# First operands loaded in pieces from two DMA queues, squares taken by pairs of tiles, outputs stored from two queues, and one GpSimd sum fewer

## The chip, the cores and the metric

The kernel runs on one core of one Trainium2 chip. The metric is device time in microseconds (us) of one execution, as a median over runs. The engines are named as the profile names them: PE (TensorE, the matrix engine), DVE (VectorE), ACT (ScalarE), POOL (GpSimd) and SP (SyncE, which here issues DMAs). PEld is the weight-load side of PE.

## The reference, cut to what matters

The input is x with 256 positions and 1024 features. The reference runs two mixers of a first block (a state-space mixer and a latent attention), a final norm, and then one layer of a second block: sparse attention and a convolution, a feed-forward part, a gate, and a last norm. Everything starts and ends with an RMS norm, and the change is at these two places:

```python
def rms_norm(x, w):
    xf = x.astype(jnp.float32)
    return (xf * lax.rsqrt(jnp.mean(xf * xf, axis=-1, keepdims=True) + RMS_EPS)).astype(x.dtype) * w
...
    for i in range(DEPTH):
        u = rms_norm(h, norm_w[i])
        y = ssd_mixer(u, ...)        # first step: u @ in_w
        h = h + y
...
    gate = jax.nn.sigmoid(rmsnorm(h, g_ple[i]) @ w_ple_gate[i])
    h = h + gate * (p[i] @ w_ple[i])
    return rmsnorm(h, g_final)
```

## The kernel before, in words

All activations are held transposed: `h` is 8 tiles of 128 features x 256 positions. A weight block is 128x1024, eight 128x128 tiles. Weights come from HBM in tiles named `raw` of up to 128x2048 (a ring of four buffers, line 176). To multiply at nearly full precision a weight is split into a rounded high part `whi` (ACT, line 182) and a remainder `wlo` (DVE, line 188), and three matmuls take the place of one. A few blocks are used whole, in plain float32 (`pj<-u,raw`). A float32 matmul shows as two PE rows, so a count in the timeline (x16) is twice that in the code.

**The start.** SP issues all DMAs, in program order: `n0` (the norm's weights, 4 KB), `h` in four pairs of tiles, and `raw` blocks of `w_si`, the first projection's weight. PE has nothing to work on yet and multiplies a tile of ones (`warm`, `WARM[0]` = 10 matmuls). The first projection does not wait for the norm: it multiplies `h` times `n0` without the factor 1/rms, and the factor is put on its result later (`r0b`). Function `first(k)` is the part of that projection that uses tile k of `h`: for k < 4 in float32 from `raw`, for k of 4 and over in three parts from `whi` and `wlo`. Meanwhile `square(k)` squares tile k on ACT and adds it to `ss` on DVE; `col_sum` sums `ss` over its 128 partitions with matmuls against ones into `st` (two matmuls, one for each half of the positions), and `mean_eps` and `rsqrt` make the factor `r0` from it on DVE, in steps on 128x2 values. `spread` turns `r0` into a tile `rb`. This stretch runs in an order written out by hand (`tc.manual_schedule`) on DVE, ACT and PE: `first(0)`, `first(1)`, `col_sum`, `first(2)`, `first(3)`, `spread`, and from there `first(4)` to `first(7)` beside the tiles `u` and their parts `uh` and `ul`. Then a scheduler orders the instructions. A side task (`dt_task`) makes small factors through a chain on DVE that ends in `av`, which PE needs for `pcum` (line 505).

**Waits on DMAs.** Each DMA signals its landing on one of eight counters, DMAHW0 to DMAHW7 in the listings, which are handed out in turn in program order over all queues. A DMA that gets a counter for the second time is issued only when the first DMA on it has landed; the queue behind it stands until then.

**`rsqrt`** is called ten times in the kernel. It starts from a guess made with integer operations (lines 257 and 258) and refines it.

**The end.** `gate_task2(m)` finishes tile m of `h` for the last norm and squares it. For m up to 6 the squares are summed on POOL (`fin.squares`, line 321) into `ssf`; tile 7 is done in two halves and its squares `sq7` go to `col_sum` themselves. On PE stand `warm` matmuls (`WARM[1]` = 6, then 1, then 6) between the `col_sum` calls, and after them come `mean_eps`, `rsqrt`, `spread`, five multiplications into `og` (line 1661) and five output DMAs from SP (line 1662).

Of the kernel before, what the change touches and what calls it, by code (L numbers as in the profile page):

```python
# [8 lines left out]
FT = mybir.dt.float32  # L9
# [7 lines left out]
S = 256  # L17
# [81 lines left out]
def build(tc, a, out):  # L99
# [54 lines left out]
    vec = const.tile([128, NVEC], FT, name="vec")  # L154
    cst = const.tile([128, NCST], FT, name="cst")
    n0 = const.tile([128, 8], FT, name="n0")
    nc.sync.dma_start(n0, a["n0"])
    nc.sync.dma_start(h[:, 0:2], a["xT"][:, 0:2])
    ones = const.tile([128, 128], FT, name="ones")
    nc.gpsimd.memset(ones, 1.0)  # L160

# [11 lines left out]
    def load(src):  # L173
        n = src.shape[-1]
        raw = wpool.tile([128, 2048], FT, name="raw", bufs=4)
        nc.sync.dma_start(raw[:, :n], src)
        return raw
# [73 lines left out]


    def rsqrt(x, n, y):
        t = small.tile([128, n], I32, name="rq_t")
        e = small.tile([128, n], FT, name="rq_e")
        c = small.tile([128, n], FT, name="rq_c")
        nc.vector.tensor_scalar(t, x.bitcast(I32), 1, None, op0=OP.logical_shift_right)
        nc.vector.tensor_scalar(y.bitcast(I32), t, -1, 0x5F3759DF, op0=OP.mult, op1=OP.add)

        nc.vector.tensor_mul(e, y, y)  # L260
        nc.vector.tensor_mul(e, e, x)
        nc.vector.tensor_scalar(e, e, 1.0, None, op0=OP.subtract)
        nc.vector.tensor_scalar(y, y, RSQRT[0], None, op0=OP.mult)
        nc.vector.scalar_tensor_tensor(c, e, RSQRT[1], e, op0=OP.add, op1=OP.mult)
        nc.vector.scalar_tensor_tensor(c, c, RSQRT[2], e, op0=OP.add, op1=OP.mult)
        nc.vector.scalar_tensor_tensor(c, c, RSQRT[3], e, op0=OP.add, op1=OP.mult)
        nc.vector.scalar_tensor_tensor(y, c, RSQRT[4], y, op0=OP.add, op1=OP.mult)

    def col_sum(o, s, start, stop=True):

        for b in range(2):
            mm(o[:, b:b + 1], s[:, b * 128:(b + 1) * 128], ones[:, 0:1], start and b == 0, stop)
# [83 lines left out]
        for _ in range(n):  # L356
            nc.tensor.matmul(p[:, :128], ones, ones, start=True, stop=True, skip_group_check=True)

    raws = [load(a["w_si"][:, :1024])]
    for i in range(1, 4):  # L360
        nc.sync.dma_start(h[:, 2 * i:2 * i + 2], a["xT"][:, 2 * i:2 * i + 2])
    raws += [load(a["w_si"][:, i * 1024:(i + 1) * 1024]) for i in (1, 2)]
# [11 lines left out]
    with tc.manual_schedule(engines={mybir.EngineType.DVE, mybir.EngineType.Activation, mybir.EngineType.PE}):  # L374
        pst = mx_ps("st")
        f0, x0, w0 = [], {}, {}
        ss = pa.tile([128, S], FT, name="ss", bufs=1)

        def square(k):
            s = ss if k == 0 else pa.tile([128, S], FT, name="sq0", bufs=2)  # L380
            nc.scalar.activation(s, h[:, k], AF.Square)
            if k:
                nc.vector.tensor_add(ss, ss, s)  # L383

# [17 lines left out]
        for k in range(4):  # L402
            u = pa.tile([128, S], FT, name="u0", tag="y", bufs=18)
            nc.vector.tensor_scalar(u, h[:, k], n0[:, k:k + 1], None, op0=OP.mult)
            f0.append(u)
            square(k)
        first(0)
        first(1)
        for k in range(4, 8):
            square(k)  # L410
        for k in range(4, 8):
            first_hi(k)
        col_sum(pst[:, :2], ss, True)
        first_lo(4)
        first_lo(5)
        m0 = small.tile([128, 2], FT, name="m0")
# [1195 lines left out]
    def gate_task2(m, p):  # L1612
# [1 line left out]
            yield 500  # L1614
        zh = pf.tile([128, S], FT, name="zh")
        if m == 7:
            last[0] = pf.tile([128, S], FT, name="sq7", bufs=1)

        for t in (slice(0, 128), slice(128, S)) if m == 7 else (slice(0, S),):
            nc.vector.scalar_tensor_tensor(zh[:, t], p[:, t], 0.5, r4b[:, t], op0=OP.mult, op1=OP.mult)  # L1620
# [3 lines left out]
            if m == 7:  # L1624
                nc.scalar.activation(last[0][:, t], h[:, m, t], AF.Square)
        done(p)
        if m < 7:
            fin.squares(m)

    last = [None]  # L1630
    w_pg = stream(a["w_pg"])
    w0 = [next(w_pg) for _ in range(4)]
    outs = four_ps(4)
# [9 lines left out]
    p = mx_ps("st")  # L1643
    warm(wp, WARM[1])
    col_sum(p[:, :2], fin.ss[0], True, False)
    warm(wp, WARM[2])
    col_sum(p[:, :2], last[0], False)
    warm(wp, WARM[3])
# [8 lines left out]
    p = mx_ps("spread")  # L1657
    spread(p, r5)
    m = 0
    for n in (1, 2, 2, 2, 1):  # L1660
        nc.vector.tensor_mul(og[:, m:m + n], og[:, m:m + n], p[:, None, :S].to_broadcast([128, n, S]))
        nc.sync.dma_start(out[:, m:m + n], og[:, m:m + n])
        m += n
    done(p)
    while pools:
# [131 lines left out]
```

## Time and profile before

| what | us |
|---|---|
| median of 3 runs | 863.78 (863.61 to 864.26) |
| the profiled execution's own time | 863.92 |
| its span in the profile | 862.0 |
| PE busy | 840.7 (98%) |
| DVE busy | 714.8 (83%) |
| ACT busy | 543.6 (63%) |
| PE busy in 0 to 20 us | 17.38 |
| PE busy in 841.5 to 862 us | 13.35 |

The span is what the profiler saw of the engines; 1.92 us of the execution's own time lie around it. Times in the sections below count from the start of the span. A busy PE is a PE with a matmul in its pipeline.

### The profile page before, as it was taken

What the parts mean: (1) busy time and instruction counts of PE and PEld (TensorE: products, weight loads), DVE (VectorE), ACT (ScalarE), POOL (GpSimd) and SP (SyncE); (2) the same over time, 40 slices, a digit from 0 to 9 for tenths busy, and PEclk for the clock granted to TensorE, in tenths of its full rate; (3) what the DMA queues carried; (4) which work ended last, traced back from release to release, by engine and by line L of the source; (5) the groups of instructions that cost most, each with busy time, mean ns of one, the idle gap of its engine ahead of it and who ended that gap; (6) DMA issues with size and microseconds to landing.
All of it is one profiled execution on the core that took longest, in us unless ns stands there. A gap on an engine that the chain in (4) does not pass through costs nothing.

```text
span 862.0 us, 17387 instructions
## 1 busy us (share of the span) xinstructions
PE 840.7 (98%) x6886; PEld 806.6 (94%) x6886; DVE 714.8 (83%) x1549; ACT 543.6 (63%) x1113; POOL 53.8 (6%) x66
## 2 busy tenths in 40 slices
PE   8999999999999999999999998998999999999996
PEld 8888999999999999999999887887999999999996
DVE  6999999788758888886679998965879988988756
ACT  5765766555647688786636465974558666656543
POOL 0000000110210000000330000001020000000102
PEclk9999999999999999999999998999999999999999
DMA  8424434444525335154343852335442655645601
GB/s 339 157 98 160 183 118 177 160 169 162 196 96 206 122 103 185 53 193 168 126 163 117 308 211 75 123 144 198 148 159 102 244 200 190 216 167 187 213 2 50
DMA packets 21681, 137.68 MB, mean 160 GB/s; under 512 B 2528, under 2 KB 3552, under 8 KB 6752
## 3 DMA queue, kind: packets, MB, share of 16 engines
q1 hardware_dynamic: 21600, 136.58, 43.7%
q8 instruction: 54, 0.88, 0.4%
q14 instruction: 27, 0.22, 0.1%
HBM read 135.52 MB, written 1.05 MB: 158 GB/s over the span
## 4 chain that ended last, share of the span: by engine, by line
PE 86%; DVE 5%; ACT 5%; DMA 1%; issue 1%; POOL 1%; SPq 0%; POOLq 0%; DVEq 0%; ACTq 0%
PE pj L146 54%; PE acc L146 10%; PE pz L146 10%; PE po L146 3%; PE ps L146 2%; DVE cv L1129 1%; ACT whi L182 1%; DVE wlo L188 1%; PE pt L150 1%; PE py L146 1%; ACT rope_t L800 1%; PE s L146 1%; DMA h<-in_xT 1%; PE pc L146 1%; DMA raw<-in_w_si 1%
## 5 line engine op out<-in xcount | busy, mean ns | idle before, releaser
L188 DVE TENSOR_TENSOR wlo<-raw,whi 128x1024 fp32r<-128x1024 f32 (+3 forms) x243 | 287.0, 1186 | 48.8 <-ACT whi L182 46.3
L182 ACT ACTIVATE whi<-raw 128x1024 fp32r<-128x1024 f32 (+3 forms) x243 | 247.0, 1025 | 108.7 <-PE pj L146 65.3
L146 PE MATMUL pj<-uh,whi 128*128 128x256 f32 x896 | 256.2, 287 | 2.6 <-DVE zh L1046 2.6
L146 PE MATMUL pj<-uh,wlo 128*128 128x256 f32 x896 | 253.6, 283 | 1.3 <-DVE wlo L188 1.2
L146 PE MATMUL pj<-ul,whi 128*128 128x256 f32 x896 | 252.8, 282 | 0.0
L146 PEld LDWEIGHTS pj<-uh,whi 128*128 128x128 f32 x896 | 169.7, 190 | 5.8 <-DVE zh L1046 2.8
L146 PEld LDWEIGHTS pj<-uh,wlo 128*128 128x128 f32 x896 | 170.1, 190 | 2.6 <-DVE wlo L188 2.1
L146 PEld LDWEIGHTS pj<-ul,whi 128*128 128x128 f32 x896 | 169.9, 190 | 0.6 <-issue 0.4
L146 PE MATMUL pz<-uh,whi 128*128 128x256 f32 x256 | 73.9, 288 | 0.4 <-ACT v L864 0.4
L146 PE MATMUL pz<-ul,whi 128*128 128x256 f32 x256 | 71.9, 281 | 0.0
L146 PE MATMUL pz<-uh,wlo 128*128 128x256 f32 x256 | 71.8, 280 | 0.0
L321 POOL TENSOR_TENSOR ss<-sqh,ss 128x256 f32<-128x256 f32 x35 | 30.1, 871 | 431.2 <-ACT sqh L320 430.7
L1129 DVE SCALAR_TENSOR_TENSOR cv<-cc,vec,cv 128x252 f32<-128x252 f32 (+28 forms) x120 | 50.0, 457 | 0.0
L146 PEld LDWEIGHTS pz<-uh,whi 128*128 128x128 f32 x256 | 48.3, 189 | 0.6 <-ACT v L864 0.6
L146 PEld LDWEIGHTS pz<-uh,wlo 128*128 128x128 f32 x256 | 48.3, 189 | 0.0
L146 PEld LDWEIGHTS pz<-ul,whi 128*128 128x128 f32 x256 | 48.2, 188 | 0.1
L1556 DVE SCALAR_TENSOR_TENSOR vo<-v,vec,vo 128x255 f32<-128x255 f32 (+1 forms) x88 | 41.7, 478 | 0.9
L534 DVE SCALAR_TENSOR_TENSOR cacc<-pj,cwh,cacc 128x253 f32<-128x253 f32 (+2 forms) x84 | 38.8, 473 | 2.2 <-ACT cacc L532 2.2
L146 PE MATMUL pj<-u,raw 128*128 128x256 f32 x128 | 31.2, 382 | 1.0 <-DMA raw<-in_w_si 1.0
L1554 ACT ACTIVATE vo<-v,vec 128x256 f32<-128x256 f32 x44 | 25.7, 590 | 3.4 <-DVE v L1551 3.3
L146 PEld LDWEIGHTS pj<-u,raw 128*128 128x128 f32 x128 | 22.9, 190 | 4.4 <-DVE ss L383 1.3
L900 ACT ACTIVATE P<-ps,nb,scq 128x128 f32<-128x128 f32 (+1 forms) x32 | 15.9, 507 | 14.7 <-DVE nb L898 14.7
(470 smaller groups left out, 2015.1 us busy)
## 6 DMA issues: line engine op xcount, KB each, us to landing
raw<-in_w_si SPq DMA_DIRECT2D x22, 1024.0 KB, 4.7
raw<-in_w_up SPq DMA_DIRECT2D x22, 1024.0 KB, 4.7
raw<-in_w_in SPq DMA_DIRECT2D x16, 1024.0 KB, 4.6
raw<-in_w_so SPq DMA_DIRECT2D x8, 1024.0 KB, 4.6
raw<-in_w_mz SPq DMA_DIRECT2D x8, 1024.0 KB, 4.6
raw<-in_w_mo SPq DMA_DIRECT2D x8, 1024.0 KB, 4.6
raw<-in_w_dn SPq DMA_DIRECT2D x8, 1024.0 KB, 4.7
raw<-in_w_mkv SPq DMA_DIRECT2D x4, 1024.0 KB, 4.7
```

What stands on the lines that cost most here:

```text
L146: nc.tensor.matmul(o, l, r, start=start, stop=stop, skip_group_check=True)
L150: nc.tensor.transpose(o, i, ident)
L182: nc.scalar.activation(hi[:, :n], raw, AF.Copy)
L188: nc.vector.tensor_sub(lo[:, :n], raw, hi[:, :n])
L321: nc.gpsimd.tensor_tensor(ss, s, ss, op=OP.add)
L534: nc.vector.scalar_tensor_tensor(acc[:, j:], p[:, :S - j], cwh[:, (3 - j) * 32 + f:(3 - j) * 32 + f + 1], acc[:, j:], op0=OP.mult, op1=OP.add)
L800: nc.scalar.activation(t[i ^ 32:(i ^ 32) + 32], src[i:i + 32], AF.Copy)
L900: nc.scalar.activation(P[:, c0:c0 + n], s[:, c0:c0 + n], AF.Exp, bias=nb[:, b:b + 1], scale=scq[:, b:b + 1], accum_out=sm[:, b:b + 1])
L1129: nc.vector.scalar_tensor_tensor(o[:, j:], c[:, :S - j], V("c31", (30 - j) * 4 + i), o[:, j:], op0=OP.mult, op1=OP.add)
L1554: nc.scalar.activation(o, v, AF.Identity, bias=V("fcb", f), scale=V("fcw", 88 + f))
L1556: nc.vector.scalar_tensor_tensor(o[:, j:], v[:, :S - j], V("fcw", (2 - j) * 44 + f), o[:, j:], op0=OP.mult, op1=OP.add)
```

## The change

The first weight block is loaded in two halves of 128x512 from ACT's DMA queue, while SP's queue starts with tile 0 of `h` instead of a pair, then `n0`, then tile 1. `square` now takes two tiles at a time, 128x512, so that four squares and three additions stand where eight and seven stood; `ss` and the squares take buffers of the later tiles `M` and `xdt`. `ss` is two tiles wide now, so `col_sum` is called twice at the start. In `rsqrt` the two integer steps become one, in all ten calls. At the end the squares of tile 6 are no longer added on POOL; they have a `col_sum` of their own. The outputs are stored from SP and ACT in turn.

```diff
--- before.py
+++ after.py
@@ -154,8 +154,13 @@
     vec = const.tile([128, NVEC], FT, name="vec")
     cst = const.tile([128, NCST], FT, name="cst")
     n0 = const.tile([128, 8], FT, name="n0")
+
+    raw0 = wpool.tile([128, 2048], FT, name="raw", bufs=4)
+    nc.scalar.dma_start(raw0[:, :512], a["w_si"][:, :512])
+    nc.sync.dma_start(h[:, 0:1], a["xT"][:, 0:1])
     nc.sync.dma_start(n0, a["n0"])
-    nc.sync.dma_start(h[:, 0:2], a["xT"][:, 0:2])
+    nc.scalar.dma_start(raw0[:, 512:1024], a["w_si"][:, 512:1024])
+    nc.sync.dma_start(h[:, 1:2], a["xT"][:, 1:2])
     ones = const.tile([128, 128], FT, name="ones")
     nc.gpsimd.memset(ones, 1.0)
 
@@ -251,11 +256,9 @@
 
 
     def rsqrt(x, n, y):
-        t = small.tile([128, n], I32, name="rq_t")
         e = small.tile([128, n], FT, name="rq_e")
         c = small.tile([128, n], FT, name="rq_c")
-        nc.vector.tensor_scalar(t, x.bitcast(I32), 1, None, op0=OP.logical_shift_right)
-        nc.vector.tensor_scalar(y.bitcast(I32), t, -1, 0x5F3759DF, op0=OP.mult, op1=OP.add)
+        nc.vector.tensor_scalar(y.bitcast(I32), x.bitcast(I32), -0.5, float(0x5F3759DF), op0=OP.mult, op1=OP.add)
 
         nc.vector.tensor_mul(e, y, y)
         nc.vector.tensor_mul(e, e, x)
@@ -356,7 +359,7 @@
         for _ in range(n):
             nc.tensor.matmul(p[:, :128], ones, ones, start=True, stop=True, skip_group_check=True)
 
-    raws = [load(a["w_si"][:, :1024])]
+    raws = [raw0]
     for i in range(1, 4):
         nc.sync.dma_start(h[:, 2 * i:2 * i + 2], a["xT"][:, 2 * i:2 * i + 2])
     raws += [load(a["w_si"][:, i * 1024:(i + 1) * 1024]) for i in (1, 2)]
@@ -374,11 +377,11 @@
     with tc.manual_schedule(engines={mybir.EngineType.DVE, mybir.EngineType.Activation, mybir.EngineType.PE}):
         pst = mx_ps("st")
         f0, x0, w0 = [], {}, {}
-        ss = pa.tile([128, S], FT, name="ss", bufs=1)
+        ss = pa.tile([128, 2, S], FT, name="ss", tag="M", bufs=3)
 
         def square(k):
-            s = ss if k == 0 else pa.tile([128, S], FT, name="sq0", bufs=2)
-            nc.scalar.activation(s, h[:, k], AF.Square)
+            s = ss if k == 0 else pa.tile([128, 2, S], FT, name="sq0", tag="xdt")
+            nc.scalar.activation(s, h[:, k:k + 2], AF.Square)
             if k:
                 nc.vector.tensor_add(ss, ss, s)
 
@@ -403,14 +406,16 @@
             u = pa.tile([128, S], FT, name="u0", tag="y", bufs=18)
             nc.vector.tensor_scalar(u, h[:, k], n0[:, k:k + 1], None, op0=OP.mult)
             f0.append(u)
-            square(k)
+            if k % 2:
+                square(k - 1)
         first(0)
         first(1)
-        for k in range(4, 8):
+        for k in (4, 6):
             square(k)
         for k in range(4, 8):
             first_hi(k)
-        col_sum(pst[:, :2], ss, True)
+        col_sum(pst[:, :2], ss[:, 0], True, False)
+        col_sum(pst[:, :2], ss[:, 1], False)
         first_lo(4)
         first_lo(5)
         m0 = small.tile([128, 2], FT, name="m0")
@@ -1614,7 +1619,7 @@
             yield 500
         zh = pf.tile([128, S], FT, name="zh")
         if m == 7:
-            last[0] = pf.tile([128, S], FT, name="sq7", bufs=1)
+            last[0] = pf.tile([128, S], FT, name="sq7", tag="sq7", bufs=2)
 
         for t in (slice(0, 128), slice(128, S)) if m == 7 else (slice(0, S),):
             nc.vector.scalar_tensor_tensor(zh[:, t], p[:, t], 0.5, r4b[:, t], op0=OP.mult, op1=OP.mult)
@@ -1624,10 +1629,13 @@
             if m == 7:
                 nc.scalar.activation(last[0][:, t], h[:, m, t], AF.Square)
         done(p)
-        if m < 7:
+        if m < 6:
             fin.squares(m)
-
-    last = [None]
+        elif m == 6:
+            last[1] = pf.tile([128, S], FT, name="sq6", tag="sq7", bufs=2)
+            nc.scalar.activation(last[1], h[:, m], AF.Square)
+
+    last = [None, None]
     w_pg = stream(a["w_pg"])
     w0 = [next(w_pg) for _ in range(4)]
     outs = four_ps(4)
@@ -1643,6 +1651,7 @@
     p = mx_ps("st")
     warm(wp, WARM[1])
     col_sum(p[:, :2], fin.ss[0], True, False)
+    col_sum(p[:, :2], last[1], False, False)
     warm(wp, WARM[2])
     col_sum(p[:, :2], last[0], False)
     warm(wp, WARM[3])
@@ -1657,9 +1666,9 @@
     p = mx_ps("spread")
     spread(p, r5)
     m = 0
-    for n in (1, 2, 2, 2, 1):
+    for i, n in enumerate((1, 2, 2, 2, 1)):
         nc.vector.tensor_mul(og[:, m:m + n], og[:, m:m + n], p[:, None, :S].to_broadcast([128, n, S]))
-        nc.sync.dma_start(out[:, m:m + n], og[:, m:m + n])
+        (nc.scalar if i % 2 else nc.sync).dma_start(out[:, m:m + n], og[:, m:m + n])
         m += n
     done(p)
     while pools:
```

At the start ACT's order, and what each row waits for, was this before:

```order
L381 ACT_TABLE_LOAD
L381 ACTIVATE ss<-h 128x256 [waits DMAHW1_49]
L381 ACTIVATE sq_127<-h 128x256
L381 ACTIVATE sq_132<-h 128x256 [waits DMAHW3_49]
L381 ACTIVATE sq_137<-h 128x256 [waits DVE_49]
L381 ACTIVATE sq_148<-h 128x256 [waits DMAHW4_49,DVE_49]
```

and is this after the change:

```order
L159 DMA raw<-in_w_si 128x512
L162 DMA raw<-in_w_si 128x512
L384 ACT_TABLE_LOAD [waits DMAHW4_49]
L384 ACTIVATE ss<-h 128x512 [waits DMAHW1_49]
L384 ACTIVATE sq_133<-h 128x512 [waits DMAHW5_49]
L384 ACTIVATE sq_144<-h 128x512 [waits DMAHW6_49]
L384 ACTIVATE sq_147<-h 128x512 [waits DMAHW7_49,DVE_49]
```

The load of ACT's function table stood first and free; it now stands behind two DMA issues and behind the wait for DMAHW4, the landing of tile 1 of `h`.

SP's first rows were these before (`n` is `n0`):

```order
L157 DMA n_76<-in_n 128x8
L158 DMA h<-in_xT 128x512
L176 DMA raw<-in_w_si 128x1024
L361 DMA h<-in_xT 128x512 x3
L176 DMA raw<-in_w_si 128x1024 x2
L363 DMA cst<-in_cst 128x384 [waits DMAHW0_49]
L176 DMA raw<-in_w_si 128x1024 [waits DMAHW1_49]
L365 DMA vec<-in_vec 128x669 [waits DMAHW2_49]
```

and these after:

```order
L160 DMA h<-in_xT 128x256
L161 DMA n_76<-in_n 128x8
L163 DMA h<-in_xT 128x256
L364 DMA h<-in_xT 128x512 x3
L181 DMA raw<-in_w_si 128x1024 [waits DMAHW0_49]
L181 DMA raw<-in_w_si 128x1024 [waits DMAHW1_49]
L366 DMA cst<-in_cst 128x384 [waits DMAHW2_49]
L181 DMA raw<-in_w_si 128x1024 [waits DMAHW3_49]
```

The next `raw` block, which was issued without a wait, now waits for DMAHW0 (the first half of the first block, from ACT's queue), and everything behind it on SP with it; the third waits for DMAHW1 (tile 0 of `h`), the fourth for DMAHW3 (the second half).

On DVE the place is the end of `first(7)`, where `pr`, the product of the first projection's result with `r0b`, waits for PE. Before:

```order
L292 TENSOR_TENSOR ul<-u,uh 128x256 [waits Activation_49]
L433 SCALAR_TENSOR_TENSOR u<-h,n_76,rb 128x256
L626 TENSOR_TENSOR pr<-pj,r0b 128x256 [waits PE_49]
L292 TENSOR_TENSOR ul<-u,uh 128x256 [waits Activation_49]
L433 SCALAR_TENSOR_TENSOR u<-h,n_76,rb 128x256
L534 SCALAR_TENSOR_TENSOR cacc<-pr,cwh,cacc 128x255 [waits Activation_49]
L626 TENSOR_TENSOR pr<-pj,r0b 128x256 [waits PE_49]
```

After:

```order
L295 TENSOR_TENSOR ul<-u,uh 128x256 [waits Activation_49]
L438 SCALAR_TENSOR_TENSOR u<-h,n_76,rb 128x256
L295 TENSOR_TENSOR ul<-u,uh 128x256 [waits Activation_49]
L438 SCALAR_TENSOR_TENSOR u<-h,n_76,rb 128x256
L631 TENSOR_TENSOR pr<-pj,r0b 128x256 [waits PE_49] x2
L295 TENSOR_TENSOR ul<-u,uh 128x256 [waits Activation_49]
L438 SCALAR_TENSOR_TENSOR u<-h,n_76,rb 128x256
```

One more tile `u` and its part `ul` stand ahead of the first `pr` now, and two `pr` stand together.

At the end of the program PE's rows were these before (`ssf` is the sum over tiles 0 to 6, `sq_11535` the squares of tile 7):

```order
L357 MATMUL warm<-ones 128x128 x6
L146 MATMUL st<-ones,ssf 128x1 x2
L357 MATMUL warm<-ones 128x128 x2
L146 MATMUL st<-ones,sq_11535 128x1
L357 MATMUL warm<-ones 128x128
L146 MATMUL st<-ones,sq_11535 128x1
L357 MATMUL warm<-ones 128x128 x4
```

and are these after (`ssf` over tiles 0 to 5, `sq_11482` the squares of tile 6, `sq_11506` those of tile 7):

```order
L360 MATMUL warm<-ones 128x128 x6
L146 MATMUL st<-ones,ssf 128x1 x2
L146 MATMUL st<-ones,sq_11482 128x1 x2
L360 MATMUL warm<-ones 128x128 x2
L146 MATMUL st<-ones,sq_11506 128x1
L360 MATMUL warm<-ones 128x128
L146 MATMUL st<-ones,sq_11506 128x1
L360 MATMUL warm<-ones 128x128 x4
```

Two matmuls for tile 6 have come in between `ssf` and the second run of `warm`; nothing has left this row.

## Rows read from the trace of the kernel before

**Rows 1.** The page's busy us by engine, and stretch 0 to 20 us by windows.
```profile
PE 840.7 (98%) x6886; PEld 806.6 (94%) x6886; DVE 714.8 (83%) x1549; ACT 543.6 (63%) x1113; POOL 53.8 (6%) x66
...
0.00:20.00 20.00, 17.38 (x101) 15.94 (x102) 12.32 (x39) 11.14 (x23) 0.41 (x5) 1.00 0.88 333
```

**Rows 2.** PE's waits, whole run: us in total, times, longest.
```profile
PE pcum L146 <- DVE av L505: 1.5, 1, 1.5
...
PE spread L146 <- DVE r L267: 1.1, 1, 1.1
```

**Rows 3.** Timeline, first 12 us: start, length, what, [idle before <-releaser].
```profile
0.73 1.28 ACT L381 ACT_TABLE_LOAD   x1 [0.73 <-PEq L1787]
...
0.74 0.37 SPq L157 DMA_DIRECT2D n<-in_n  x1
...
0.99 4.64 PE L357 MATMUL warm<-ones 128*128 128x128 f32 x20 [0.99 <-POOL ones L160]
1.17 0.42 SPq L158 DMA_DIRECT2D h<-in_xT  x1
1.63 0.42 SPq L176 DMA_DIRECT2D raw<-in_w_si  x1
2.10 1.38 SPq L361 DMA_DIRECT2D h<-in_xT  x3
...
6.67 3.69 PE L146 MATMUL pj<-u,raw 128*128 128x256 f32 x16 [1.05 <-DMA raw<-in_w_si]
...
10.95 0.61 PE L146 MATMUL st<-ones,ss 128*128 128x1 f32 x4 [0.59 <-DVE ss L383]
...
11.42 3.70 PE L146 MATMUL pj<-u,raw 128*128 128x256 f32 x16
```

**Rows 4.** DMAs issued at 1.17, 1.63, 3.52 and 3.05: count, size, us to landing.
```profile
h<-in_xT SPq DMA_DIRECT2D x1, 256.0 KB, 3.9
...
raw<-in_w_si SPq DMA_DIRECT2D x1, 512.0 KB, 4.9
...
raw<-in_w_si SPq DMA_DIRECT2D x1, 512.0 KB, 6.4
h<-in_xT SPq DMA_DIRECT2D x1, 256.0 KB, 5.6
```

**Rows 5.** The 128x512 forms, ACT by line and DVE by line: busy us, mean ns.
```profile
L581 ACT ACTIVATE M<-pl 128x512 f32<-128x512 f32 x16 | 8.8, 593 | 6.1 <-PE pl L146 6.0
...
L584 DVE TENSOR_TENSOR M<-M,cb 128x512 f32<-128x512 f32 x16 | 10.6, 684 | 0.7 <-ACT M L583 0.3
```

**Rows 6.** Timeline around PE's wait for pcum, and DVE and ACT before it.
```profile
20.73 0.42 DVE L626 TENSOR_TENSOR pr<-pj,r0b 128x256 f32<-128x256 f32 x1 [0.89 <-PE pj L146]
...
39.52 1.06 ACT L182 ACTIVATE whi<-raw 128x1024 fp32r<-128x1024 f32 x1 [0.58 <-DMA raw<-in_w_si]
```

**Rows 7.** Timeline of the end, up to the second step of the last rsqrt.
```profile
849.95 1.50 PE L357 MATMUL warm<-ones 128*128 128x128 f32 x12
...
851.51 0.52 PEld L146 LDWEIGHTS st<-ones,ssf 128*128 128x128 f32 x4 [0.25 <-POOL ssf L321]
...
851.98 0.69 PE L357 MATMUL warm<-ones 128*128 128x128 f32 x4
...
852.95 0.28 PE L146 MATMUL st<-ones,sq 128*128 128x1 f32 x2
...
852.04 0.51 ACT L1625 ACTIVATE sq<-h 128x128 f32<-128x128 f32 x2 [1.06 <-DVE h L1623]
...
853.47 0.17 DVE L257 TENSOR_SCALAR rq_t<-m 128x2 int32<-128x2 int32 x1
853.67 0.17 DVE L258 TENSOR_SCALAR r<-rq_t 128x2 int32<-128x2 int32 x1
```

**Rows 8.** Line 1662, the output DMAs: ns min/median/max, first and last start.
```profile
L1662 SPq DMA_DIRECT2D out_dram<-og x5: 332/344/412, 856.6 to 858.8; - x5
...
DMA to landing us min/median/max: 1.9/2.2/2.2
```

## The prediction

> **What bounds the kernel now.** I read the busy times first: PE works 840.7 us of a span of 862.0 [rows 1], so time can only come from the 21 us in which PE has nothing to do, or from what PE does needlessly. The change touches the two ends, so I read those in order of time.
>
> In the first 20 us PE is busy for 17.38 [rows 1], and the timeline shows where the other 2.62 lie: 0.99 before its first warm matmul, 1.05 before `first(0)` (a DMA of `raw` is late) and 0.59 before `col_sum` (the sum `ss` on DVE is late) [rows 3]. Behind 10.95 PE does not stop in this stretch. The reader is to see there that the warm matmuls end at 0.99 + 4.64 = 5.63, `first(0)` and `first(1)` take 3.69 from 6.67 on, the four rows of `st` take 0.47 (10.95 to 11.42), and `first(2)` starts at 11.42. So the start can give 1.05 + 0.59 = 1.64 at most.
>
> At the end PE's rows stand close: twelve warm rows from 849.95, `st` from 851.51, more warm rows from 851.98, the last `st` at 852.95 [rows 7]. Before the first `st` the weight load sat idle for 0.25 us, put down to POOL's sum. The squares of tile 7 are ready at 852.04 + 0.51 = 852.55, ahead of the `st` at 852.95 that needs them: here PE's own queue sets the time, not ACT or DVE. Behind it come the steps of `rsqrt`, then the output, whose last DMA starts at 858.8 and lands about 2.2 later [rows 8].
>
> **The landings.** From the issue times [rows 3] and the times to landing [rows 4], 260 KB (`n0` and the first pair of `h`) are in at 1.17 + 3.9 = 5.07, 772 KB (`raw` too) at 1.63 + 4.9 = 6.53, and 1540 KB (all of `h`) at 3.05 + 5.6 = 8.65; 3.05 is the third of the three issues that fill 1.38 from 2.10. I call the time between straight. After the change the same bytes go out, but the first big transfers leave in the slot at 0.74 and not at 1.17, so I move all of it by 0.43. I let the two queues share alike. Tile 1 and the first half of the weight block are then in when 516 KB are: 5.07 + 256/512 of 1.46 = 5.80, less 0.43, 5.37. Tiles 2 and 3 and the second half: 1028 KB, 6.53 + 256/768 of 2.12 = 7.24, less 0.43, 6.81. All of `h`: 8.22.
>
> On this the Trainium skill has a rule that speaks against the change ("DMA: Bandwidth & Descriptors", section "Rules for kernel authors"): spreading DMAs over SP and ACT does not raise the bandwidth, because both feed the same engines, and only saves issue time. By it nothing but the slot of 0.43 is won, as in my shift.
>
> **The start, part by part.** *Weights in halves.* With the first half in at 5.37 and warm-up ending at 5.63, `first(0)` starts at about 5.63 and not 6.67, and both parts end at 5.63 + 3.69 = 9.32. The second half, in at 6.81, is needed at 5.63 + 1.85 = 7.48, so it hides.
>
> *The table load.* ACT's function table took 1.28 us from 0.73 on, beside the wait for `h`, and cost nothing [rows 3]. In the listing after the change it stands behind the wait for tile 1. Its cover is gone: it runs from 5.37 to 6.65 and the first square behind it. The next block of `raw`, too, has a wait it did not have.
>
> *Squares by pairs.* The kernel has no 128x512 square from SBUF in the trace; the nearest is a 128x512 activation at 0.593, and for the sum the 128x512 product at 0.684 [rows 5]. The second square ends at 6.65 + 2 x 0.593 = 7.84, its tiles being in at 6.81. From there three additions at 0.684 follow on DVE, 9.89; the third and fourth square end at 8.43 and about 9.1 (the fourth waits for the first addition's buffer, free at 8.52, and for `h` at 8.22), so the additions run back to back. With 0.1 for handing over, `col_sum` starts at 10.0 and not 10.95. PE waits 0.7 for it.
>
> *Two `col_sum` for one.* PE's four `st` rows take 0.47; now there are eight, 0.94. `first(2)` starts at 10.0 + 0.94 = 10.94 and not 11.42: **0.48 less.** From both sides: with no wait at all PE gets there at 9.32 + 0.94 = 10.26, 1.16 less; if tile 1 comes only with 772 KB and without the shift, at 6.53, everything is 1.16 later, 12.10, 0.68 more.
>
> *The next block.* It used to be issued at 3.52 and land 6.4 later, 9.92; PE took it at 11.42. Now SP holds it until the first half is in, 5.37, when by the count above over half of `h` is still to come. If it simply follows `h`, it lands at 8.22 + 1.46 (what 512 KB took between 5.07 and 6.53) = 9.7, before 10.94. If it needs 6.4 again, 11.8, and the gain becomes a loss of 0.4. I take 9.7, since its 6.4 were a queue behind the 1540 KB that are the same now.
>
> *Carrying it on.* Further on PE waits once for DVE, 1.5 us for `pcum` [rows 2]. DVE's chain to it comes from the same start and shifts with it; I let the gain of 0.48 pass unchanged.
>
> **rsqrt.** Of ten calls only one makes PE wait for its result, `spread` at the end [rows 2]; the others hide under PE's matmuls and give nothing (without that cover each would give one step). A step is 853.67 - 853.47 = 0.20 [rows 7], which the last call saves.
>
> **The end.** POOL's sum of tile 6 goes, and with it the idle 0.25. In its place PE has four more `st` rows on its path: 0.47. With the step of `rsqrt`: + 0.47 - 0.25 - 0.20 = **0.02 more.** Tile 7's squares come earlier too, but they were not awaited. The output DMAs on two queues: the last one stays on SP, and its issue at 858.8 waits for its data rather than for SP, since five issues of 0.34 [rows 8] have more than 2 us to be done in. I take nothing; at best it lands in 1.9 as the fastest did, 0.3 less. If POOL's idle is not won back, it is 0.25 more.
>
> **Sum:** - 0.48 + 0.02 = - 0.46. The profiled execution took 863.92, 0.14 over the median of 863.78. So 863.46 for it, and 863.3 for the median.
>
> **The rivals.** A measurement of this kernel can tell about 0.2%, 1.7 us, from no change.
>
> *It is faster by more* (17%). `h` comes sooner and PE's waits go altogether, 1.16 less; and PE is not what counts there but DVE, which used to idle 0.89 ahead of `pr` [rows 6] and now has a `u` and an `ul` to do in that time, so that `pcum`'s 1.5 us shrink by 0.89 as well. With 0.28 at the end (0.3 less 0.02) that is 2.3 less, 861.5. For it: the order of DVE. Against it: ACT's split at 39.52 waits for a DMA [rows 6] whose buffer PE has to free, so DVE cannot run ahead of PE past there.
>
> *The gain is used up* (20%). Tile 1 lands near 5.9, or PE's gain only lengthens the wait for `pcum`, and the time stays at 863.8.
>
> *The table load costs more than its row* (10%). Its row was never followed at once by an activation, so the trace does not show what comes with it; I take twice its 1.28. Then `col_sum` moves 1.28 later, and the time is 864.6. The Trainium skill ("ScalarE: Activation LUTs", section "What ACT_TABLE_LOAD costs") gives 1283 ns, as this row has, and a drain of 1380 ns besides, which no row here shows; by it the sum would be 864.7, an estimate from that page.
>
> *It is slower, because SP stands* (8%). Suppose ACT's queue is served behind SP's: then the first half comes with 4 + 1024 + 256 = 1284 KB, 7.94 less 0.43, 7.5. SP's next block goes out only then, and with 6.4 to landing PE has it at 13.9 and not at 11.42: 2.5 more, 866.2. It decides for slower by the bound from a landing of the first half at 6.75 on (6.75 + 6.4 = 11.42 + 1.73). For it: the wait in SP's order. Against it: the first half is the first transfer of its queue, and the first pair of `h`, second in its own, took 3.9 [rows 4].
>
> **How the numbers follow.** The forecast, between 862.9 and 863.7, has 45%. Faster by over 0.2% is the first rival, 0.17; slower the last, 0.08; the rest, 0.75, lies within. The range from 862.0 to 864.8 takes in the forecast, the used-up gain, the dear table load, and the bounds of start and end (863.78 - 1.16 - 0.28 = 862.3, and 863.78 + 0.68 + 0.27 = 864.7), and leaves out most of the first and all of the last rival.
>
> **What would show it.** Right: the table load stands at about 5.4 and the first square behind 6.6; `first(0)` starts at 5.6 to 5.7; `st` at about 10.0 with eight rows and 0.94 to `first(2)`; at the end eight `st` rows without a wait and the last one some 0.2 later after the last `pj` than now; the output's last landing unchanged. Wrong: a square that starts before tile 1 is in, `first(2)` waiting for `raw`, or a `pcum` wait that has grown by the start's gain or shrunk by more than 0.3. The forecast fails if the landings do not share alike, on which both 5.37 and 8.22 rest.

## The result, and the profile after

The changed kernel takes 870.03 us (median of 6 runs, 867.14 to 871.98), the kernel before 863.69 beside it (6 runs, 862.43 to 864.26). The ratio is 1.0065, 95% interval 1.0049 to 1.0081: slower by 0.65%, where I had forecast 863.3. The profiled execution took 871.98, the longest of the six, with a span of 869.9; what follows is read from it.

The page's busy times, in the form of [rows 1]:

```profile
PE 848.0 (97%) x6894; PEld 813.5 (94%) x6894; DVE 712.1 (82%) x1534; ACT 543.4 (62%) x1109; POOL 52.9 (6%) x65
```

PE is the thing to look at: eight matmuls more, and 7.3 us more of busy time. Eight column-sum matmuls do not take 7.3 us, so PE ran slower somewhere. The timeline of the first 20 us shows the first place (start, length, what, idle before):

```profile
0.73 0.41 ACTq L159 DMA_DIRECT2D raw<-in_w_si  x1
...
2.10 1.38 SPq L364 DMA_DIRECT2D h<-in_xT  x3
4.31 0.80 SPq L181 DMA_DIRECT2D raw<-in_w_si  x2
...
5.12 3.62 PE L146 MATMUL pj<-u,raw 128*128 128x256 f32 x16
...
5.56 1.28 ACT L384 ACT_TABLE_LOAD   x1 [5.56 <-DMA h<-in_xT]
...
6.85 0.63 ACT L384 ACTIVATE ss<-h 128x512 f32<-128x512 f32 x1
...
8.97 1.38 ACT L384 ACTIVATE sq<-h 128x512 f32<-128x512 f32 x2 [0.97 <-DMA h<-in_xT]
9.63 1.49 DVE L386 TENSOR_TENSOR ss<-ss,sq 128x512 f32<-128x512 f32 x2 [0.90 <-ACT sq L384]
...
11.17 1.49 PE L146 MATMUL st<-ones,ss 128*128 128x1 f32 x8 [2.43 <-DVE ss L386]
...
12.52 6.62 PE L146 MATMUL pj<-u,raw 128*128 128x256 f32 x16
...
18.98 0.61 PE L146 MATMUL rb<-cst,r 128*128 128x128 f32 x4
```

`first(0)` starts 1.55 earlier than in [rows 3], but PE then waits 2.43 for the sum of squares. Behind that wait the same sixteen matmuls of `first(2)` and `first(3)` that took 3.70 take 6.62. The windows of that stretch say why (the column behind PE's busy time is the granted clock, the last two are DMA share and GB/s):

```profile
8.00:10.00 2.00, 0.74 (x4) 1.00 0.91 338
10.00:12.00 2.00, 0.83 (x6) 0.90 1.03 409
12.00:14.00 2.00, 2.00 (x8) 0.50 1.04 405
14.00:16.00 2.00, 2.00 (x6) 0.50 1.07 433
16.00:18.00 2.00, 2.00 (x6) 0.50 0.62 262
18.00:20.00 2.00, 2.00 (x13) 0.89 0.01 4
```

A granted clock of 1.00 is TensorE's 2.4 GHz, 0.50 its 1.2 GHz: behind the wait it works at half speed until past 18 us. `rb` comes at 18.98 where the kernel before has it at 14.96, 4.02 later.

The second place is less visible. By 834 us the changed kernel is 8.1 behind, and no other wait of PE has grown by more than 0.1. What differs is the distance between matmuls in a row, that is, from the start of one to the start of the next. Near 805 us, in the down projection of the feed-forward part, kernel before:

```profile
804.73 0.28 PE L146 MATMUL pj<-fh,whi 128*128 128x256 f32 x1
...
805.07 0.28 PE L146 MATMUL pj<-fh,whi 128*128 128x256 f32 x1
```

and the changed kernel, which executes the same matmuls there:

```profile
804.92 0.28 PE L146 MATMUL pj<-fl,whi 128*128 128x256 f32 x1
...
805.28 0.28 PE L146 MATMUL pj<-fl,whi 128*128 128x256 f32 x1
```

From the first row to the last, two left out between, there are three steps. They take 0.34 before and 0.36 after, 113 and 120 ns each, at a granted clock of 1.00 in both. The program has 528 such matmuls with `fh` and `fl`; at 6 to 7 ns each that is some 3.5 us at most. Not every matmul became slower: those of `oh` and `ol` (the attention output) near 425 us stand 117 ns apart before (six steps in 0.70) and 113 ns near 430 us in the changed kernel (six in 0.68).

The end, which answers to [rows 7]:

```profile
857.88 1.50 PE L360 MATMUL warm<-ones 128*128 128x128 f32 x12
859.22 0.50 PE L146 MATMUL st<-ones,ssf 128*128 128x1 f32 x4
859.58 0.58 PE L146 MATMUL st<-ones,sq 128*128 128x1 f32 x4
...
861.00 0.28 PE L146 MATMUL st<-ones,sq 128*128 128x1 f32 x2
861.15 1.14 PE L360 MATMUL warm<-ones 128*128 128x128 f32 x8
863.21 0.68 PE L146 MATMUL spread<-cst,r 128*128 128x128 f32 x4 [0.92 <-DVE r L270]
```

From the first warm-up matmul to the first of `spread` it takes 5.33 (before 5.41), and from there to the end of the span 6.65 in both. So the end is as long as it was.

### The profile page after: what moved, and what is told of

It is laid out like the page before. It is cut to its first block, busy times and chain, and to the rows that moved or that the text cites. A ratio compares the mean times of both kernels' runs of the same rounds, so it can differ in the third digit from the quotient of the medians.

```text
span 869.9 us, 17382 instructions
## 1 busy us (share of the span) xinstructions
PE 848.0 (97%) x6894; PEld 813.5 (94%) x6894; DVE 712.1 (82%) x1534; ACT 543.4 (62%) x1109; POOL 52.9 (6%) x65
## 3 DMA queue, kind: packets, MB, share of 16 engines
q10 hardware_dynamic: 576, 1.05, 0.3%
HBM read 135.52 MB, written 1.05 MB: 157 GB/s over the span
## 4 chain that ended last, share of the span: by engine, by line
PE 88%; ACT 5%; DVE 4%; DMA 1%; issue 1%; POOL 0%; SPq 0%; DVEq 0%; ACTq 0%; POOLq 0%
PE pj L146 55%; PE acc L146 10%; PE pz L146 10%; PE po L146 2%; PE ps L146 2%; ACT whi L187 1%; DVE cv L1134 1%; PE pt L150 1%; DVE wlo L193 1%; PE py L146 1%; ACT rope_t L805 1%; PE s L146 1%; DMA h<-in_xT 1%; PE st L146 1%; PE pc L146 1%; DMA raw<-in_w_si 1%
## 5 line engine op out<-in xcount | busy, mean ns | idle before, releaser
L146 PE MATMUL pj<-u,raw 128*128 128x256 f32 x128 | 33.7, 408 | 0.0
L146 PEld LDWEIGHTS pj<-u,raw 128*128 128x128 f32 x128 | 25.2, 207 | 3.6
```

The source lines that it names most:

```text
L146: nc.tensor.matmul(o, l, r, start=start, stop=stop, skip_group_check=True)
```

## The experiments

Kernels of one group ran on one chip with the same runs of the kernel before. "rq_t" is the small tile that the two-step `rsqrt` wrote to and that the change drops.

| kernel | us, median (runs) | ratio to before, 95% |
|---|---|---|
| new start only | 865.65 (10) | 1.0008 [0.9994, 1.0023] |
| short rsqrt and new end only | 869.14 (5) | 1.0052 [1.0036, 1.0068] |
| whole change, wait filled | 870.48 (4) | 1.0067 [1.0052, 1.0082] |
| squares by pairs only | 863.32 (10) | 0.9989 [0.9979, 0.9998] |
| short rsqrt only, rq_t kept | 863.90 (10) | 0.9996 [0.9987, 1.0005] |
| two-step rsqrt, rq_t gone | 869.55 (4) | 1.0067 [1.0050, 1.0084] |
| whole change, rq_t kept | 865.77 (10) | 1.0015 [1.0003, 1.0028] |
| before, `uh` and `ul` 32 bytes lower | 867.08 (4) | 1.0038 [1.0023, 1.0053] |
| whole change, wait filled, rq_t kept | 863.92 (10) | 0.9999 [0.9989, 1.0009] |
| before, wait of 1.9 made | 865.66 (4) | 1.0021 [0.9999, 1.0043] |
| before, tiles behind small's head 64 higher | 869.79 (4) | 1.0072 [1.0057, 1.0087] |
| the same, 32 higher | 867.81 (4) | 1.0045 [1.0030, 1.0060] |
| before, `uh` and `ul` 96 lower | 863.27 (10) | 0.9991 [0.9976, 1.0007] |
| before, tiles behind small's head 128 higher | 867.32 (10) | 1.0035 [1.0024, 1.0047] |
| before, all but `uh` and `ul` 64 higher | 869.67 (4) | 1.0063 [1.0039, 1.0088] |
| before, wait of 3.4 made | 868.96 (5) | 1.0050 [1.0031, 1.0070] |
| change without pieces, rq_t kept, more warm-up | 864.59 (12) | 1.0001 [0.9992, 1.0010] |
| the same, `uh` and `ul` 96 lower | 862.63 (11) | 0.9983 [0.9974, 0.9991] |

**Which part costs it.** My first theory was the start alone: the long wait and the half clock behind it. The rival was a cost in the end. Four kernels divide the change: the start without the rest, the rest without the start, the whole with ten warm-up matmuls in the wait, and only the squares by pairs.

```diff
+        wg = mm_ps("warm")
+        warm(wg, 10)
+        done(wg)
         col_sum(pst[:, :2], ss[:, 0], True, False)
```

> The start of the changed kernel (pieces from two queues, squares by pairs, two column sums) with rsqrt and the end as before. Theory of the gap: in the changed kernel PE stood still for 2.43 us ahead of the column sum, and behind that its granted clock was 0.50 from about 11.6 to 18.4 us, so that first(2) and first(3) took 6.5 us instead of 3.5; all of the loss is then in the start, and this kernel shows it whole: a gap of 2 to 2.6 us, a clock of 0.50 behind it, pcum at 49 to 50 us instead of 45.5, a time 3.5 to 8 us over that of before. Rival of the drift: the loss lies in the matmuls later on (they stood 117 ns apart before and 119 ns in the changed kernel between 640 and 830 us), and has to do with the end or with rsqrt; then this kernel stays within 2 us of before.

> The start as before, with the shorter rsqrt and the end of the changed kernel (squares of tile 6 to a column sum of their own, output DMAs from two queues). Theory of the gap: nothing at the start changes, pcum at 45.5 us, and the end gives 0.0 to 0.3 us by the rows of the changed kernel (the last rsqrt 0.2 shorter, the column sums 0.1 longer): 863.4 to 863.7. Rival of the drift: 3 us or more slower than before, with matmuls 119 ns apart late in the run.

> The changed kernel, with 10 warm matmuls (20 rows, about 2.3 us) on PE between first(1) and the column sum, where it stood still. Theory of the gap: the sum still comes at about 11.1, but the granted clock stays at 1.00, first(2) starts at 12.1 and first(2) and first(3) take 3.5 to 3.7; pcum at 46.3 to 46.9 us instead of 49.7, and the time falls by about 3 us against the changed kernel. Rival of the supply: the clock is not the cause but late operands (raw blocks and the factor rb); pcum stays at 49 to 50 us and the time as it was, or rises by what the matmuls take.

> The kernel before with squares by pairs and the two column sums alone: loads from SP as before, rsqrt and end as before. The table load has no wait ahead of it. Theory of the gap: first(0) starts at 6.7 as before and ends with first(1) at 10.4, the sum comes at about 10.0 to 10.3, so PE hardly waits, the clock stays at 1.00, and first(2) starts at 11.3 to 11.4 (0.59 of waiting won, 0.47 for the second column sum lost): 863.5 to 863.9. Rival: pairs by themselves make the sum late (each square of a pair needs both tiles); then PE waits over 1.5 us ahead of the column sum and the time is 2 us or more over that of before.

The theory fell as a whole account: the start alone costs 0.08%, not to be told from nothing, while the rest alone, which leaves the start as it was, costs 0.52%. The start is not free in every execution, though: seven of its ten runs, from 864.8 to 867.1, have a mean granted clock of 0.992 to 0.994, and three, from 863.0 to 863.5, one of 0.996. The profiled one is of the three, and behind its wait of 1.69 the clock stays at 1.00. And the theory was right on the clock in the changed kernel. With the wait filled, PE's timeline of that kernel reads

```profile
8.66 2.40 PE L360 MATMUL warm<-ones 128*128 128x128 f32 x20
10.90 0.95 PE L146 MATMUL st<-ones,ss 128*128 128x1 f32 x8
11.71 3.70 PE L146 MATMUL pj<-u,raw 128*128 128x256 f32 x16
```

so `first(2)` has its 3.70 back, and `pcum` is 0.8 later than before in place of 4.1. It still ends slow, with the wide distances between matmuls of the changed kernel: 870.48, where I had expected about 3 us less than the changed kernel's 870.03. The squares by pairs alone do what I reckoned: `st` at 10.44, no wait of PE for it, `first(2)` at 11.36.

**Instructions or addresses.** The kernels with wide distances (whole change, short `rsqrt` and end, wait filled) have one thing in common that no row shows: rq_t is gone. Its three buffers of 32 bytes stood in the pool `small`, and in the built program everything allocated behind it lies 96 bytes lower; `fh` goes from byte 138496 of its partition to 138400. Four kernels tell the addresses from the instructions: one step with the tile kept, two steps with the tile gone,

```diff
-        t = small.tile([128, n], I32, name="rq_t")
         e = small.tile([128, n], FT, name="rq_e")
         c = small.tile([128, n], FT, name="rq_c")
+        t = c.bitcast(I32)
```

the whole change with the tile kept (`small.tile([128, n], I32, name="rq_t")` alone, never written), and 32 bytes of padding behind `ul`, the last of the tiles that lie from the other end of SBUF.

> Kernel before with the one-step rsqrt, but the tile rq_t stays allocated, so that every tile lies at the address that it has in the kernel before. Address theory (the 4 us that the end-only version loses over the whole run come from tiles that move down 96 bytes in SBUF once rq_t is gone, which takes fh, fl and gh from a multiple of 64 bytes to 32 bytes off one): 863.0 to 864.5, ratio within 0.2% of the kernel before, and the spacing of the fh,whi matmuls from 800 us on is 110 ns in two of the three passes, as before. Theory that the one-step rsqrt itself costs it: 868 to 870. Theory that the new end costs it: no loss here, and none in the next run either.

> Kernel before with its two-step rsqrt, whose first step now writes into the tile rq_c instead of a tile of its own: the same instructions on each engine, and all tiles behind rq_t lie 96 bytes lower, as in the changed kernel. Address theory: 867 to 869.5 (ratio about 1.005), the fh and fl matmuls at 119 to 120 ns in all three passes where the kernel before has 110, 120, 110. One-step theory and new-end theory: 863 to 864.5.

> The whole changed kernel, with rq_t still allocated. Address theory: the later loss is gone and only the start is left: 863.3 (as I predicted) in executions where TensorE's clock does not fall after the wait for the sum of squares, about 867 where it does (rb later by 4.0); between those in the median. Theory that the end or the one-step rsqrt costs it: 868 to 870 as the changed kernel.

> Kernel before with 32 bytes of padding behind ul, so that uh and ul lie 32 bytes lower, on multiples of 64 bytes, where they are 32 bytes off in both kernels; nothing else moves. Address theory in its simple form (a moving operand that starts on a multiple of 64 bytes is read faster): the 3456 matmuls of uh and ul go from a spacing of about 118 ns to about 113 to 115, 10 to 17 us less: 847 to 854. If the address of these two tiles does not matter, or only that of whi or wlo beside them: 863 to 864.5.

The first two settle it. The kernel with the one-step `rsqrt` and the old addresses is at 0.9996, and the kernel with the old instructions and the new addresses at 1.0067, as slow as the whole change. The latter's trace has the instructions of the kernel before in the same order on every engine, so a changed schedule is not the cause. Their rows at 805 us, first with the tile kept:

```profile
805.14 0.28 PE L146 MATMUL pj<-fh,whi 128*128 128x256 f32 x1
...
805.48 0.28 PE L146 MATMUL pj<-fh,whi 128*128 128x256 f32 x1
```

and with it gone, otherwise as before:

```profile
804.97 0.28 PE L146 MATMUL pj<-fh,whi 128*128 128x256 f32 x1
...
805.32 0.29 PE L146 MATMUL pj<-fh,whi 128*128 128x256 f32 x1
```

Again three steps each: 0.34 and 0.35. The whole change with the tile kept is 4.3 faster than without. Ten runs of it show what is left: two, at 862.65 and 863.08, have a mean clock of 0.998 and 0.996, and eight, from 865.0 to 866.8, one of 0.993 to 0.995. The profiled one is of the eight; its windows (PE alone) show the half clock for a shorter time than above, behind a wait of 1.52:

```profile
10.00:12.00 2.00, 1.60 (x9) 0.78 1.03 411
12.00:14.00 2.00, 2.00 (x6) 0.50 1.03 401
14.00:16.00 2.00, 2.00 (x9) 0.87 1.06 431
```

The padding behind `ul` was a miss: I had expected 847 to 854, and `uh` and `ul` on multiples of 64 bytes cost 0.38%, so my simple form of the rule (a multiple of 64 is fast) is wrong.

**Both repairs, the wait made, and the dose.** One kernel has both repairs. One makes the wait in the kernel before, by work on VectorE that changes nothing:

```diff
+        for _ in range(4):
+            nc.vector.tensor_scalar(ss, ss, 1.0, None, op0=OP.mult)
         col_sum(pst[:, :2], ss, True)
```

Two move the tiles of the kernel before up, by a padding tile as the first in `small`.

> The whole changed kernel with both repairs: rq_t stays allocated, and ten more warm-up matmuls stand ahead of the sum of squares, so that TensorE has work in the wait for the last h tiles. Theory of two causes (half clock after that wait, and tile addresses): nothing of the loss is left, 863.0 to 864.3; every execution shows a clock of 0.996 or more where the version with rq_t alone had 0.993 in most; st at about 10.9, first(2) in 3.7 us, fh and fl matmuls at 110 to 115 ns. If there is a third cause in the change: 865 or more.

> Kernel before, in which VectorE multiplies the sum of squares by 1.0 four times before TensorE may sum it (four instructions of 128x256, about 0.5 us each in a row): the wait of TensorE before st goes from 0.59 to about 2.6 us, and nothing else is changed, no transfer and no queue. Theory that the idle time itself brings the clock down: granted clock 0.50 for several us from st on, first(2) and first(3) take 5 to 6.5 us where they took 3.5, rb 4 to 6 us later, 867 to 870. Rival (the low clock came from the pieces, the second queue or the extra column sum): first(2) in 3.7 us, rb and the end 2.0 later: 865.5 to 866.3.

> Kernel before with 64 bytes of padding at the head of the pool small: the same tiles move as when rq_t goes, but by 64 bytes, so that fh, fl, gh stay on multiples of 64 bytes (and cease to be on multiples of 128). If the place within 64 bytes decides: 863 to 864.5, same as before, fh at 110 to 115 ns. If it is the distance to whi and wlo, or any move at all: 866 to 870.

> The same with 32 bytes of padding: fh, fl and gh are 32 bytes off a multiple of 64. If the place within 64 bytes decides: 867 to 870 as with rq_t gone, fh and fl at 119 to 120 ns. If it is the particular move by 96 bytes down that cost: 863 to 864.5.

With both repairs the change is at 0.9999, with no run above 865.0: no third cause is needed for this kernel. The made wait came out shorter than meant, 1.90, since the four multiplications took 0.32 each and not 0.5. In its profile the clock stays at 1.00 behind that wait, and with four runs the time is not to be told from that of the kernel before:

```profile
12.12 0.61 PE L146 MATMUL st<-ones,ss 128*128 128x1 f32 x4 [1.90 <-DVE ss L414]
12.59 3.70 PE L146 MATMUL pj<-u,raw 128*128 128x256 f32 x16
```

Both paddings cost, 0.72% with 64 bytes and 0.45% with 32. So the place within 64 bytes, which a move by 64 keeps, does not decide it either.

**What of the address, and a longer wait.** Two questions were left: whether a place within 128 bytes fits, or the distance to the weights' tiles, and whether an idle PE alone lowers its clock. Two kernels take the paddings on (24 words behind `ul`, 32 words in `small`), one has 16 words ahead of `raw`, and one makes eight multiplications of the four.

> Kernel before with 96 bytes of padding behind ul, so that uh and ul lie on multiples of 128 bytes; nothing else moves. Theory of 128 bytes (absolute place, or distance to the weights): the matmuls of uh and ul go from about 118 ns to 113 to 115 where TensorE does not wait for weights, 3456 of them, at most 3456 x 4.5 ns = 15 us less: 849 to 858. Theory that these tiles are held by something else (weights that arrive at that rate): 863 to 864.5.

> Kernel before with 128 bytes of padding at the head of the pool small. Theory of 128 bytes: nothing changes, 863 to 864.5, fh and fl at 110 to 115 ns. Theory that any move off the first addresses costs: 867 to 870.

> Kernel before with 64 bytes of padding ahead of raw, whi and wlo, so that everything but uh and ul moves by 64 bytes together: the distance of fh, fl, gh to the weights stays, their place within 128 bytes is that of the version with 64 bytes at the head of small. Absolute place: 868 to 870, fh and fl at 119 to 120 ns. Distance to the weights: fh and fl stay at 110 to 115 ns, 863 to 865.

> Kernel before with eight multiplications by 1.0 instead of four between the last sum of squares and TensorE's column sum: the wait before st about 3.1 us. Theory that the idle time brings the clock down: 0.50 for some 6 us from 13 us on, first(2) takes 5 to 6.5 us, 868 to 870. If a wait of 3.1 us leaves the clock at 1.00: 866 to 867, and something else of the changed start is the cause.

The wait is settled. Nothing but eight multiplications on VectorE was added to the kernel before, PE waited 3.36 in the profiled run, and from 14 to 18 us its granted clock was 0.50:

```profile
13.52 1.01 PE L146 MATMUL st<-ones,ss 128*128 128x1 f32 x4 [3.36 <-DVE ss L414]
14.39 6.27 PE L146 MATMUL pj<-u,raw 128*128 128x256 f32 x16
20.50 0.61 PE L146 MATMUL rb<-cst,r 128*128 128x128 f32 x4
```

`rb` is 5.5 later, of which 2.6 are the wait made longer and the rest the half clock.

The address rule is not. A move by 128 bytes, which keeps every place within 128, costs 0.35%, so places within 128 alone do not decide. A move of everything but `uh` and `ul` by 64 bytes leaves the matmuls of `fh` and `fl` at 113 ns, as before, and slows those of `uh` and `ul` from 118 to 120 ns. That fits the distance to the weights' tiles, though the weights' own place has moved too. But with only `uh` and `ul` moved by 96 bytes, the matmuls of `fh` became slower in the profiled run, 118 ns, and none of their own tiles had moved; in the last kernel below, with the same padding, they are at 113 ns again. So either the distance differs between executions of one layout, or something besides these addresses bears on it; no run here tells which. The gain of up to 15 us that the theory of 128 bytes allowed did not come: the ten runs of that kernel lie at 861.0 to 863.3 and at 865.1 to 865.9, and in the profiled one, of 865.81, the clock fell behind a wait of 1.94 ahead of `first(0)`. No rule that I have fits all seven moves. What they do show is the scatter: with unchanged instructions (one padding write on GpSimd apart) the same kernel lies between 0.9991 and 1.0072 of itself.

**Is a gain left?** Two kernels keep the pairs, the one-step `rsqrt` and the new end, drop the pieces, and fill PE's first idle time (`WARM = (16, 6, 1, 6)` for `(10, 6, 1, 6)`).

> Changed kernel without the pieces (first loads as before), with rq_t still allocated and 16 warm-up matmuls instead of 10 ahead of the first operands, which fill the idle time of 1.0 to 1.8 us there. Squares by pairs, the one-step rsqrt and the new end stay. If the parts gain what their steps showed (pairs -0.3 at the first scan, the sum of squares at the end -0.9 before the last output DMAs, rsqrt -0.2): 862.5 to 863.3, ratio 0.998 to 0.9995, and fewer executions above 865 than the kernel before has. If they are lost in what follows them: 863.7 to 864.3.

> The same with 96 bytes of padding behind ul. The version with that padding alone fell into two groups of times, 861.0 to 863.3 and 865.1 to 865.9, and its profile of 865.8 had the clock down at the start. If the extra warm-up matmuls hold the clock there and the two changes add: 861 to 863 with few above. If the two groups come from elsewhere: 861 to 866 as there.

At the old addresses nothing is left, 1.0001; in its profile the clock was down once more, between 68 and 74 us. With `uh` and `ul` moved it is 0.17% faster than the kernel before, 862.63, the fastest here. That is a gain found by trying addresses, and not by the change: from 1.0001 to 0.9983 only these two tiles moved. The same move without the rest is at 0.9991, not to be told from nothing, so what it is worth is open.

## Why the prediction was wrong, point by point

The changed kernel took 6.7 more than I had forecast. I looked for time in PE's idle 21 us and in needless work, and so took PE's own pace as fixed; both losses are in the main a slower pace. In the terms of the sum, two steps failed. `rsqrt` had one step of 0.20 and nothing for the addresses, which cost 0.67% by themselves. The start's 0.48 less rested on all of `h` at 8.22, which came at 9.65, and on a wait of PE counted at its own length, 0.7, which was 2.43. `first(2)` came 1.10 later than before, at 12.52, and behind that wait its and `first(3)`'s matmuls took 2.92 more.

- **First operands: right, and more.** I had the first half in at 5.37 and `first(0)` at 5.63; it started at 5.12, because the halves landed 3.6 and 4.0 after their issue, and the warm-up was through before the 5.63 that I had counted. The landings did not share alike, on which I had rested them: the first half was in at 0.73 + 3.6 = 4.33, and tile 1, by the table load that waits for it, at 5.56, where I had both at 5.37.
- **The table load: right.** It stands at 5.56, and the first square follows at 6.85, at once behind its 1.28. The drain of 1380 ns that the Trainium skill ("ScalarE: Activation LUTs", section "What ACT_TABLE_LOAD costs") adds to it is not to be seen here, so the rival built on twice the price falls.
- **Squares by pairs, two column sums: right in size.** The rows of the result give 0.63 and 0.69 for a square and 0.75 for an addition, where I had 0.593 and 0.684. With the pairs alone `st` to `first(2)` took 0.92, where I had 0.94.
- **All of `h` at 8.22: this is the step that failed at the start.** The three issues from 2.10 on landed after

```profile
DMA to landing us min/median/max: 4.0/6.4/6.6
```

  where the last of them took 5.6 in [rows 4]. The last pair was in at 3.05 + 6.6 = 9.65. The rates by windows (granted clock, DMA share, GB/s) show that more was moved at first and less from 6 us on; before, then after:

```profile
4.00:5.00 1.00, 1.00 0.91 272
...
7.00:8.00 1.00, 1.00 1.07 418
8.00:9.00 1.00, 1.00 1.05 432
```

```profile
4.00:5.00 1.00, 1.00 1.04 372
...
7.00:8.00 1.00, 1.00 1.15 231
8.00:9.00 1.00, 1.00 0.83 289
```

  Between 2 and 9 us the DMA engines moved 1.97 MB, and 2.10 before: the first pieces came sooner and the last pair of `h` later. So the bytes did not come straight one behind the other, as I had called them; why the last pair came late, no run here shows. The Trainium skill's rule that I quoted ("DMA: Bandwidth & Descriptors", section "Rules for kernel authors") says that a second queue adds no bandwidth, and these sums agree. So the last squares waited 0.97 for `h`, `st` came at 11.17 and not at 10.0, and PE's wait was 2.43 and not 0.7. In the kernel with the new start alone it was 1.69: the landings differ from run to run.
- **What a wait costs: missed.** I counted a wait at its own length. In this kernel it can cost several us more, and the kernel before shows it in rows that I did not look for:

```profile
521.92 0.58 PE L146 MATMUL pj<-uh,whi 128*128 128x256 f32 x1 [2.58 <-DVE zh L1046]
```

```profile
520.00:522.00 2.00, 0.08 (x1) 0.82 0.00 0
522.00:524.00 2.00, 1.90 (x7) 0.50 0.00 0
524.00:526.00 2.00, 2.00 (x12) 0.50 0.34 66
```

  That half clock is in the 863.92 of the profiled execution already. It is not in every execution: of the 20 profiled ones, one of each kernel here, 17 have it behind this wait, and in three the clock stays at 1.00, as in the kernel with both repairs:

```profile
523.07 0.39 PE L146 MATMUL pj<-uh,whi 128*128 128x256 f32 x1 [2.59 <-DVE zh L1055]
```

```profile
522.00:524.00 2.00, 0.78 (x3) 1.00 0.00 0
524.00:526.00 2.00, 1.80 (x15) 1.00 0.00 0
```

  The new start added a second, in some runs: the change moved PE's idle time, which had stood in two parts of 1.05 and 0.59, into one of 1.5 to 2.4.
- **The next block, and carrying it on to `pcum`: right, for a loss.** `first(2)` followed `st` without a wait for `raw`. What passed on was not a gain but the delay: 4.02 at `rb` and 4.1 at `pcum`, whose own wait was 1.3 for 1.5.
- **`rsqrt`: the step is right, the tile was missed.** The last call is one step of 0.20 shorter. I had nothing for the 96 bytes by which everything behind rq_t moves, and by the runs they are the larger part of the loss: 1.0067 alone, of 1.0065 for the whole change. The start's part is 1.0015 (the whole change with the tile kept). The two together would be 1.0082, just past the upper end of the interval measured, so the split is rough. Two of the six runs of the changed kernel, at 867.14 and 867.59, have a mean clock of 0.997 and 0.995; the other four, from 869.71 to 871.98, have 0.991 to 0.994.
- **The end: right.** I had 0.02 more; the rows above give 0.08 less up to `spread` and nothing behind it.

One thing does not add up: filling the wait gained 1.9 us at the old addresses and, by the medians, nothing at the new ones, though the profiles show the clock held at the start in both. The profiled executions at the new addresses differ by 1.6 (870.41 and 871.98). I have no run that tells why.

## What to carry to other kernels

Before a first-load change is counted as a gain, see where the idle time goes: several short waits of PE may be cheaper than one long wait, and a few matmuls of no use in it can hold the clock. When a tile is dropped or resized, compare the addresses of everything behind it, or keep the space; in a kernel like this one, a difference of half a per cent otherwise says nothing of the edit itself. A comparison of two versions is worth repeating with some padding before one believes it.

## What the runs showed of the hardware

- TensorE's granted clock fell to 0.50 behind idle times of 2.43, 2.58 and 3.36 us, and `first(2)` with `first(3)` then took 6.62 and 6.27 where they take 3.70. The length of the wait alone does not decide: behind 1.90 it stayed at 1.00 in the one profile, behind 1.69 too, but behind 1.94 and 1.52 it fell, and behind the same wait of 2.6 near 520 us it fell in 17 profiled executions and not in three. What decides is open.
- The distance of 128x256 matmuls in a row was 113 ns in one layout of SBUF and 120 in another, at a granted clock of 1.00 and with the same instructions. Moves of 32 to 128 bytes changed the whole kernel by -0.1% to +0.7%, and some matmuls became faster by a move that slowed others. The cause is not found.
- From 7 to 9 us of the changed start the DMA engines had a busy share of 0.83 to 1.15 at 231 to 289 GB/s, and of 1.05 to 1.07 at 418 to 432 before; from 4 to 5 us they moved 372 GB/s, and 272 before. So a busy share near 1 went with quite different rates.
